# First norm's scale and bias moved from the end of the gate/up loop to units 3 to 6, on VectorE alone, and w_down's preparation two to three units later

## The chip, the cores and the metric

One core of a Trainium2 chip runs the whole program. The metric is the device time of one execution in microseconds (us). Engines are named as the profile names them: PE is TensorE's matmuls and PEld its weight loads, DVE is VectorE, ACT is ScalarE, POOL is GpSimd, SP is SyncE, which here only issues DMAs (SPq in rows).

## The reference, cut to what matters

```python
def _layernorm(x, g, b):
    mu = mean(x); var = mean((x - mu) ** 2)
    return (x - mu) * rsqrt(var + LN_EPS) * g + b
...
x = _layernorm(DN_ALPHA * x + gate_m * mix, ln1_g, ln1_b)
h = x * (1.0 + scale_f) + shift_f
ff = (silu(h @ w_gate) * (h @ w_up)) @ w_down
x = _layernorm(DN_ALPHA * x + gate_f * ff, ln2_g, ln2_b)
```

There are 2048 tokens of width 1024 in float32; the inner width of the last product pair is 2816 (22 times 128). What the change moves is two pieces of this: `* ln1_g + ln1_b` on the residual (the `x` of the last line; the `h` that feeds the products gets its scale elsewhere), and the preparation of `w_down`.

## The kernel before, in words

**Products.** Every float32 matrix is split in two float16 halves (`split`, or a copy on ACT and a subtraction on DVE), and a product is three matmuls (`mm3`, L135 to L137). The large products go by a seven-product scheme (Strassen-Winograd), so weights and activations are also added and subtracted block by block before the split, mostly on POOL.

**The gate/up loop** (`for q in range(2, NFF)`, units 0 to 21, 128 of the 2816 columns each). Unit q calls `gu` twice: `gu(q, 1)` for the second half of the tokens, then `gu(q, 0)` for the first. I call these the unit's first and second half. Each is seven products of 12 matmuls; PE runs them as A11, S2, S1, A12 and A22 (in either order), S3, S4. First halves use the PSUM tiles `mm`, second halves `ax`, four banks each. DVE's L1459 has to be done before product S3, which adds into the same bank; L1469 reads that bank after S3, L1471, L1472, L1474 and L1476 finish the half, and L1480 stores it to DRAM (`uscr`) on SP's queue. Beside the products, unit q loads the weights of unit q+3 (`gu_load`, L1384), takes the maxima of those of unit q+2 (`gu_max`, L87 into `m`), scales them (`gu_scale`) and splits those of unit q+1 (L1406, L1407, L1420, L1421). The halves' weights are held twice, so a split has a whole unit before it is needed.

**w_down** passes twice through one page of SBUF (`wd_stage["pg"]`). First `wd_load` and `wd_max` for each of 11 pieces of 1 MB (L1494, and L87 into `wdm`): three pieces per unit in units 4 to 7. After the last of them `wd_scale` reduces the 11 maxima and those of `gfrow` (L1504), and needs a maximum over the partitions for it: `all_max` lays the column out by a matmul with the identity (L99) and reduces that on DVE (L104). Then `wd_split` runs once per unit, in units 8 to 18: a multiply (L1516), four POOL additions (L1517 to L1520), two copies on ACT (L1523), two subtractions on DVE (L1524), and seven stores to `wscr` (L1526). A piece is loaded again for this.

**The first norm's scale and bias.** The normalized rows lie in DRAM as eight pieces of 1 MB (`yscr[j]`), without `ln1_g` and `ln1_b`. `y_gain(j)` loads a piece, multiplies on DVE (L1611), adds on POOL (L1612) and stores it back. Two of the eight are called in unit 19, six in unit 20. The last stage reads them as the residual.

**What sets the order.** Instructions of one engine and issues of one DMA queue run in the order in which they stand there. That order is made when the program is built, by a scheduler with its own idea of times; it moves an instruction ahead of others whose inputs come later. `with tc.high_priority()` (in `scale_of`) puts a chain first. `tc.issue_after(ins)` keeps what is issued in its block behind `ins` on `ins`'s engine: with the store of a half, a load may not pass this store on SP's queue. Otherwise the scheduler hoists: w_down's first pass of before runs in units 1 to 3, as its loads wait for nothing.

**The last stage** (after the loop) multiplies by w_down, adds into the residual and does the second norm.

Of the kernel before, what the change touches and what calls it, by code (L numbers as in the profile page):

```python
# [18 lines left out]
P = 128  # L19
T = 2048  # L20
D = 1024
# [5 lines left out]
NFF = 22  # L27
NCH = 11
# [12 lines left out]
def kernel(ctx: ExitStack, tc: tile.TileContext, xT, x, c, adaN, adaT, ada_b, w_ret, w_conv,  # L41
                             conv_w, w_out, ln1, ln1c, w_gu, w_dn, ln2, rope, consts, out):
    nc = tc.nc
# [13 lines left out]
    def page(dt=F32, at=0):  # L57


        t = unused.pop(max(-len(unused), min(at, len(unused) - 1)))  # L60
        v = t if dt == F32 else t.bitcast(dt)
        owner[id(v)] = (v, t)
        return v

    def free(*views):
        for v in views:
            unused.append(owner.pop(id(v))[1])

    def t2k(dt=F32):
        count[0] += 1  # L70
        return tmp.tile([P, 516 if dt == F32 else 1032], dt, tag="t2k", name=f"t2k{count[0]}")
# [14 lines left out]
    def absmax(dst, src):  # L86
        return nc.vector.tensor_reduce(dst, src, axis=AX.X, op=OP.max, apply_absolute_value=True).ins  # L87
# [45 lines left out]
    def mm3(ps, l_hi, l_lo, r_hi, r_lo, start, stop, again=False):  # L133

        nc.tensor.matmul(ps, l_hi, r_hi, start=start, stop=False, skip_group_check=again)  # L135
        nc.tensor.matmul(ps, l_hi, r_lo, start=False, stop=False, skip_group_check=again)  # L136
        return nc.tensor.matmul(ps, l_lo, r_hi, start=False, stop=stop, skip_group_check=again).ins  # L137
# [938 lines left out]
    for t in range(4, NT):  # L1076
        p = t // 2 + 1
# [91 lines left out]
    for b in range(2):  # L1169
        for u in range(6):  # L1170
            n = 6 * b + u
# [79 lines left out]
    def ln_rows(src):  # L1251
        pg = page()
        nc.sync.dma_start(pg.rearrange("p (a n) -> p a n", a=2),
                          bass.AP(tensor=src.tensor, offset=src.offset, ap=[[0, P], [D, 2], [1, D]]))
        return pg
# [61 lines left out]
    def plane_view(b, pl):  # L1317
        return planes[b][pl].rearrange("p (j a k n) -> p j a k n", j=4, a=2, k=4)
# [60 lines left out]
    gu_pages = ([], [], [])  # L1379
    s32 = []  # L1380
# [46 lines left out]
    def gu_done(q):  # L1427
        wa, ws = gu_w.pop(q)["pages"]
        gu_pages[0].append(wa)
        gu_pages[1].append(ws)  # L1430

    u32, ucount = [], [0]
    uscr = [[dram.tile([2, P, NCH, 512], F32, name=f"uscr{b}{r}") for r in range(2)] for b in range(2)]
    um = const.tile([P, 2, NFF], F32, name="um")

    def gu(q, bl, between=None):

        w = gu_w[q]
        iv_g, iv_u = gu_iv[q][:, 0:1], gu_iv[q][:, 1:2]
        if not u32:  # L1440
            u32.append(page())
        u = u32[0].rearrange("p (f h n) -> p f h n", f=2, h=2)[:, ucount[0] % 2]
        new = (bank, aux)[ucount[0] % 2]
        ucount[0] += 1

        def prod(ps, a, pl, start, stop):
            b = plane_view(bl, pl)
            o = ps.rearrange("p (j n) -> p j n", n=P)
            for k in range(4):
                mm3(o, w[a][:, 0, k], w[a][:, 1, k], b[:, :, 0, k], b[:, :, 1, k],  # L1450
                    start and k == 0, stop and k == 3, not start)

        pa, pb, pc = new(), new(), new()
        p1, u2 = t2k()[:, :512], t2k()[:, :512]
        e5 = w["tmp"]
        prod(pa, "A11", B11, True, True)
        nc.scalar.activation(p1, pa, AF.Copy)
        prod(pb, "S2", T2, True, True)
        nc.vector.tensor_add(u2, pb, p1)  # L1459
        prod(pc, "S1", T1_, True, True)  # L1460
        nc.scalar.activation(e5, pc, AF.Copy)
        if between:
            between()
        prod(pa, "A12", B21, False, True)
        nc.scalar.activation(u[:, 0], pa, AF.Silu, scale=iv_g)
        pd = new()
        prod(pd, "A22", T4, True, True)
        prod(pb, "S3", T3, False, True)
        nc.vector.tensor_add(p1, pb, p1)  # L1469
        nc.gpsimd.tensor_add(e5, e5, p1)  # L1470
        nc.vector.tensor_add(p1, pd, p1)  # L1471
        nc.vector.scalar_tensor_tensor(u[:, 0], p1, iv_u, u[:, 0], op0=OP.mult, op1=OP.mult)  # L1472
        prod(pc, "S4", B22, False, True)
        nc.vector.tensor_add(u2, pc, u2)  # L1474
        nc.scalar.activation(u[:, 1], u2, AF.Silu, scale=iv_g)  # L1475
        nc.vector.scalar_tensor_tensor(u[:, 1], e5, iv_u, u[:, 1], op0=OP.mult, op1=OP.mult)  # L1476

        absmax(um[:, bl, q:q + 1], u.rearrange("p h n -> p (h n)"))
        r, k = divmod(q, NCH)
        nc.sync.dma_start(uscr[bl][r][:, :, k].rearrange("h p n -> p h n"), u)  # L1480

# [5 lines left out]
    wd_stage = {}  # L1489

    def wd_load(k):
        if "pg" not in wd_stage:
            wd_stage["pg"] = page()
        nc.sync.dma_start(wd_stage["pg"], w_dn[k])  # L1494
# [14 lines left out]
    def wd_split(k):  # L1509
        if "out" not in wd_stage:  # L1510
            wd_stage["out"] = page(F16)
        f = wd_stage["pg"].rearrange("p (s n) -> p s n", s=4)
        sv = s32[0].rearrange("p (s n) -> p s n", s=4)
        o = wd_stage["out"].rearrange("p (s a n) -> p s a n", s=4, a=2)
        v = wd_stage["pg"].rearrange("p (r n) -> p r n", r=2)
        nc.vector.tensor_mul(v, v, gfrow[:, None, :].to_broadcast([P, 2, D]))  # L1516
        nc.gpsimd.tensor_sub(sv[:, 0], f[:, 1], f[:, 0])  # L1517
        nc.gpsimd.tensor_sub(f[:, 1], f[:, 3], f[:, 1])
        nc.gpsimd.tensor_sub(sv[:, 1], f[:, 3], sv[:, 0])
        nc.gpsimd.tensor_sub(sv[:, 2], f[:, 2], sv[:, 1])  # L1520
        for src, ms in ((f, (0, 6, 1, 2)), (sv[:, :3], (4, 5, 3))):
            n = len(ms)
            nc.scalar.activation(o[:, :n, 0], src, AF.Copy)  # L1523
            nc.vector.tensor_sub(o[:, :n, 1], src, o[:, :n, 0])  # L1524
            for i, m in enumerate(ms):
                nc.sync.dma_start(wscr[m][k // 4, :, k % 4], o[:, i])  # L1526
# [19 lines left out]
    def p2_xload(b, quad, c):  # L1546
        h, r = HALVES[quad]
        X[b, quad, c] = page()
        nc.sync.dma_start(X[b, quad, c].rearrange("p (k n) -> p k n", k=4)[:, :width(c)],
                          uscr[b][r][h, :, 4 * c:4 * c + width(c)])  # L1550
# [54 lines left out]


    def y_gain(j):
        pg = gu_pages[2].pop(0)
        v = pg.rearrange("p (a n) -> p a n", a=2)
        nc.sync.dma_start(v, yscr[j].rearrange("a p n -> p a n"))  # L1610
        nc.vector.tensor_mul(v, v, lnp1[0][:, None, :D].to_broadcast([P, 2, D]))  # L1611
        nc.gpsimd.tensor_add(v, v, lnp1[0][:, None, D:].to_broadcast([P, 2, D]))  # L1612
        nc.sync.dma_start(yscr[j].rearrange("a p n -> p a n"), v)
        gu_pages[2].append(pg)

    def p2_add(ps, b, m, p):
        for h, n in INTO[m]:
# [30 lines left out]
    lnp1, lnp2 = [], []  # L1648
# [77 lines left out]
    def p2_ahead(i, n, f):  # L1726
        while ns[i] < min(n, len(steps)):
            f(*steps[ns[i]])
            ns[i] += 1

    for q in range(2, NFF):
        end = q == NFF - 1
        if end:
            free(*gu_pages[0], *gu_pages[1], *gu_pages[2], *s32, *lnp1)
            for c in range(3):
                p2_xload(1, 11, c)
            p2_ahead(1, 3, p2_wload)
        gu(q, 1)
        if end:
            free(*planes[1].values())  # L1740
            for quad in (22, 21):
                for c in range(3):
                    p2_xload(1, quad, c)
        else:
            gu_split1(q + 1)
            gu_split2(q + 1, nc.gpsimd)
            if q + 3 < NFF:
                gu_load(q + 3)
            if q + 2 < NFF:
                gu_max(q + 2)  # L1750
                gu_scale(q + 2)
        if q == 3:
            wd_load(0)
        for k in range(3 * (q - 4), min(3 * (q - 4) + 3, NCH)) if q >= 4 else ():
            wd_max(k)
            wd_load((k + 1) % NCH)
            if k == NCH - 1:
                wd_scale()
        if 8 <= q < 8 + NCH:
            wd_split(q - 8)  # L1760
            if q < 7 + NCH:
                wd_load(q - 7)
        if q == NFF - 3:
            free(wd_stage["pg"], wd_stage["out"])
            gu_pages[2].append(page())
            lnp1.append(ln_rows(ln1))
        if q == NFF - 3:
            for j in (4, 5):
                y_gain(j)
        if q == NFF - 2:  # L1770
            for j in (6, 7, 0, 1, 2, 3):
                y_gain(j)
        gu(q, 0, (lambda: (p2_scale(1), p2_ahead(0, 2, p2_split))) if end else None)
        gu_done(q)
    free(*planes[0].values(), *gu_pages[0][-1:], *gu_pages[1][-1:], *u32)
    for h in range(2):
        for i in range(2):
# [116 lines left out]
```

## Time and profile before

| | us |
|---|---|
| median of 3 runs | 2124.27 (2122.6 to 2130.06) |
| the profiled execution | 2129.92 |
| its span, first to last instruction | 2128.1 |
| PE busy in it | 2026.9 (95%) |
| DVE / POOL / ACT busy | 1461.7 / 953.9 / 666.7 |

The rows of the trace come from this one execution; 1.8 us of its time lie outside its span. A row of the timeline has the start, the duration, the engine and line, what is written and read, and in brackets how long the engine idled before it and what ended this. The page's list by fortieths of the span shows where PE has gaps: near the start, around 900 us, and from 1600 to 1700 us.

### The profile page before, as it was taken

To read this page: it belongs to the slowest core of one execution; us is meant where nothing else is said; L and a number is where in the kernel's file an instruction comes from. 1 tells how busy PE (TensorE), PEld (TensorE's weight loads), DVE (VectorE), ACT (ScalarE), POOL (GpSimd) and SP (SyncE) were. 2 spreads that over 40 slices of the span, in tenths; PEclk is the share of its full clock that TensorE was granted. 3 is DMA by queue.
4 is the path that set the end of the run, shared out by engine and by line. 5 is a ranking of instruction groups with operands and counts; after the bars stand their busy time and mean duration, and the time that the engine had idled before them with its cause. 6 is when DMAs were issued, how large, how long until landed. Compare 5 with 4: busy or idle time off the path is not lost.

```text
span 2128.1 us, 24625 instructions
## 1 busy us (share of the span) xinstructions
PE 2026.9 (95%) x9631; PEld 949.7 (45%) x9631; DVE 1461.7 (69%) x1769; ACT 666.7 (31%) x728; POOL 953.9 (45%) x759
## 2 busy tenths in 40 slices
PE   8899898989899999799999999999999899999998
PEld 4355444444444544344444444444444344444443
DVE  7899556667677577768745677777767454378564
ACT  5522443424322222323323233333432122122210
POOL 3554655555742277733312344444447333134232
PEclk9999999999999999999999999999999999999999
DMA  9047454586684288765411234343345874475311
GB/s 375 25 136 237 129 159 109 150 263 190 219 315 168 82 236 200 176 180 205 149 50 60 98 131 144 126 141 134 135 167 203 298 309 175 157 271 189 149 71 78
DMA packets 189492, 361.06 MB, mean 170 GB/s; under 512 B 118080, under 2 KB 118080, under 8 KB 166592
## 3 DMA queue, kind: packets, MB, share of 16 engines
q1 hardware_dynamic: 181168, 344.55, 48.3%
q10 hardware_dynamic: 8208, 14.95, 2.0%
q8 instruction: 75, 1.23, 0.2%
q14 instruction: 41, 0.34, 0.0%
HBM read 231.26 MB, written 100.93 MB: 156 GB/s over the span
## 4 chain that ended last, share of the span: by engine, by line
PE 47%; DVE 5%; POOL 4%; DMA 4%; issue 2%; ACT 1%; SPq 0%; POOLq 0%; DVEq 0%; ACTq 0%
PE ax L135 8%; PE ax L136 8%; PE ax L137 8%; PE mm L135 8%; PE mm L136 8%; PE mm L137 8%; DMA pg<-in_w_dn_dram 1%; POOL pg L1612 1%; DMA pg<-yscr 1%; DMA yscr<-pg 1%; DVE wdm L87 1%; ACT pg L1272 1%; DVE pg L1611 1%; DVE pg L1335 1%; POOL pg L1336 1%
## 5 line engine op out<-in xcount | busy, mean ns | idle before, releaser
L135 PE MATMUL mm<-pg,pg 128*128 128x512 f16 x1604 | 608.6, 381 | 23.2 <-ACT pg L1420 8.2
L136 PE MATMUL mm<-pg,pg 128*128 128x512 f16 x1604 | 611.1, 381 | 0.0
L137 PE MATMUL mm<-pg,pg 128*128 128x512 f16 x1604 | 610.2, 381 | 0.5 <-DVE pg L889 0.5
L135 PE MATMUL ax<-pg,pg 128*128 128x512 f16 x1220 | 463.1, 380 | 12.4 <-DVE pg L1301 2.9
L136 PE MATMUL ax<-pg,pg 128*128 128x512 f16 x1220 | 463.2, 380 | 0.0
L137 PE MATMUL ax<-pg,pg 128*128 128x512 f16 x1220 | 461.6, 380 | 0.6 <-DVE pg L889 0.6
L135 PEld LDWEIGHTS <-pg 128*128 128x128 f16 x2888 | 284.1, 98 | 362.9 <-DMA pg<-pg 16.0
L136 PEld LDWEIGHTS <-pg 128*128 128x128 f16 x2888 | 284.1, 98 | 356.1 <-issue 30.4
L137 PEld LDWEIGHTS <-pg 128*128 128x128 f16 x2888 | 283.9, 98 | 350.3 <-issue 18.8
L1470 POOL TENSOR_TENSOR pg<-pg,t2k 128x512 f32<-128x512 f32 x44 | 57.9, 1317 | 328.6 <-DVE x L114 194.0
L131 DVE SCALAR_TENSOR_TENSOR pg<-pg,p2s,pg 128x2048 f16<-128x2048 f32 (+1 forms) x42 | 92.7, 2216 | 138.1 <-ACT pg L130 138.0
L130 ACT ACTIVATE pg<-pg,p2s 128x2048 f16<-128x2048 f32 (+1 forms) x42 | 77.5, 1858 | 262.3 <-PE mm L136 114.1
L1407 DVE TENSOR_TENSOR pg<-pg,pg 128x2048 f16<-128x2048 f32 x22 | 50.3, 2286 | 69.8 <-ACT pg L1406 69.8
L87 DVE TENSOR_REDUCE m<-pg 128x2 bf16<-128x2048 f32 (+1 forms) x38 | 86.3, 2276 | 16.2 <-DMA pg<-in_w_gu_dram 10.0
L525 PE MATMUL mm<-pg,pg 128*128 128x512 f16 x384 | 91.1, 393 | 5.6 <-DVE pg L533 2.5
L1475 ACT ACTIVATE pg<-t2k,ivg 128x512 f32<-128x512 f32 x44 | 31.5, 716 | 174.3 <-DVE t2k L1474 174.3
L1523 ACT ACTIVATE pg<-pg 128x2048 f16<-128x2048 f32 (+1 forms) x22 | 37.3, 1697 | 107.8 <-DMA wscr<-pg 69.6
L1524 DVE TENSOR_TENSOR pg<-pg,pg 128x2048 f16<-128x2048 f32 (+1 forms) x22 | 44.4, 2016 | 38.8 <-ACT pg L1523 38.8
L131 DVE SCALAR_TENSOR_TENSOR pg<-pg,hs,pg 128x1024 f16<-128x1024 f32 x32 | 48.5, 1535 | 29.2 <-ACT pg L130 29.0
L1264 POOL TENSOR_SCALAR rs<-mv 128x1 f32<-128x1 f32 x32 | 30.5, 957 | 82.2 <-DVE mv L1262 79.6
L1577 POOL TENSOR_TENSOR pg<-pg,pg 128x2048 f32<-128x2048 f32 (+1 forms) x6 | 26.9, 4490 | 82.0 <-DVE pg L131 38.6
L525 PEld LDWEIGHTS <-pg 128*128 128x128 f16 x384 | 38.0, 101 | 53.8 <-issue 10.0
(278 smaller groups left out, 2834.6 us busy)
## 6 DMA issues: line engine op xcount, KB each, us to landing
pg<-wscr SPq DMA_DIRECT2D x28, 1024.0 KB, 5.0
pg<-in_w_gu_dram SPq DMA_DIRECT2D x22, 1024.0 KB, 4.8
uscr<-pg SPq DMA_DIRECT2D x44, 512.0 KB, 2.7
pg<-in_w_dn_dram SPq DMA_DIRECT2D x22, 1024.0 KB, 5.8
pg<-in_adaT_dram SPq DMA_DIRECT2D x21, 1024.0 KB, 7.2
wscr<-pg SPq DMA_DIRECT2D x77, 256.0 KB, 2.9
yscr<-pg SPq DMA_DIRECT2D x16, 1024.0 KB, 4.9
pg<-uscr SPq DMA_DIRECT2D x16, 1024.0 KB, 6.5
```

Of the source, the lines that this page charges most:

```text
L87: return nc.vector.tensor_reduce(dst, src, axis=AX.X, op=OP.max, apply_absolute_value=True).ins
L130: nc.scalar.activation(hi, src, AF.Copy, scale=s)
L131: nc.vector.scalar_tensor_tensor(lo, src, s, hi, op0=OP.mult, op1=OP.subtract)
L135: nc.tensor.matmul(ps, l_hi, r_hi, start=start, stop=False, skip_group_check=again)
L136: nc.tensor.matmul(ps, l_hi, r_lo, start=False, stop=False, skip_group_check=again)
L137: return nc.tensor.matmul(ps, l_lo, r_hi, start=False, stop=stop, skip_group_check=again).ins
L525: nc.tensor.matmul(ps, hv[:, a, k, o], w[:, k], start=n == 0 and k == k0, stop=n == 2 and k == k1 - 1)
L1407: nc.vector.tensor_sub(wa[:, 2048:], pg, wa[:, :2048])
L1470: nc.gpsimd.tensor_add(e5, e5, p1)
L1475: nc.scalar.activation(u[:, 1], u2, AF.Silu, scale=iv_g)
L1523: nc.scalar.activation(o[:, :n, 0], src, AF.Copy)
L1524: nc.vector.tensor_sub(o[:, :n, 1], src, o[:, :n, 0])
```

## The change

`y_gain` now works in one page of its own (with a second page for `ln1`'s rows), does all four passes on DVE (a multiply and an addition for each half of the piece, 128x1024), and is called twice per unit in units 3 to 6: once behind the store of the unit's first half, once behind that of its second half (`tc.issue_after(gu_last[0])`). w_down's maxima are taken in units 7 to 9 (four, four and three), each load behind the store of the half before it; its splits run in units 10 to 20.

```diff
-    u32, ucount = [], [0]
+    u32, ucount, gu_last = [], [0], [None]
...
-        nc.sync.dma_start(uscr[bl][r][:, :, k].rearrange("h p n -> p h n"), u)
+        gu_last[0] = nc.sync.dma_start(uscr[bl][r][:, :, k].rearrange("h p n -> p h n"), u).ins
...
     def y_gain(j):
-        pg = gu_pages[2].pop(0)
-        v = pg.rearrange("p (a n) -> p a n", a=2)
+        v = lnp1[1].rearrange("p (a n) -> p a n", a=2)
         nc.sync.dma_start(v, yscr[j].rearrange("a p n -> p a n"))
-        nc.vector.tensor_mul(v, v, lnp1[0][:, None, :D].to_broadcast([P, 2, D]))
-        nc.gpsimd.tensor_add(v, v, lnp1[0][:, None, D:].to_broadcast([P, 2, D]))
+        for a in range(2):
+            nc.vector.tensor_mul(v[:, a], v[:, a], lnp1[0][:, :D])
+            nc.vector.tensor_add(v[:, a], v[:, a], lnp1[0][:, D:])
         nc.sync.dma_start(yscr[j].rearrange("a p n -> p a n"), v)
-        gu_pages[2].append(pg)
...
-            free(*gu_pages[0], *gu_pages[1], *gu_pages[2], *s32, *lnp1)
+            free(*gu_pages[0], *gu_pages[1], *gu_pages[2], *s32, wd_stage["pg"], wd_stage["out"])
...
-        if q == 3:
-            wd_load(0)
-        for k in range(3 * (q - 4), min(3 * (q - 4) + 3, NCH)) if q >= 4 else ():
+        with tc.issue_after(gu_last[0]):
+            if q == 3:
+                lnp1.extend((ln_rows(ln1), page()))
+            if 3 <= q < 7:
+                y_gain((4, 6, 0, 2)[q - 3])
+        for k in range(4 * (q - 7), min(4 * (q - 7) + 4, NCH)) if q >= 7 else ():
             wd_max(k)
-            wd_load((k + 1) % NCH)
+            with tc.issue_after(gu_last[0]):
+                wd_load((k + 1) % NCH)
             if k == NCH - 1:
                 wd_scale()
-        if 8 <= q < 8 + NCH:
-            wd_split(q - 8)
-            if q < 7 + NCH:
-                wd_load(q - 7)
-        if q == NFF - 3:
-            free(wd_stage["pg"], wd_stage["out"])
-            gu_pages[2].append(page())
-            lnp1.append(ln_rows(ln1))
-        if q == NFF - 3:
-            for j in (4, 5):
-                y_gain(j)
-        if q == NFF - 2:
-            for j in (6, 7, 0, 1, 2, 3):
-                y_gain(j)
+        if 10 <= q < 10 + NCH:
+            wd_split(q - 10)
+            if q < 9 + NCH:
+                wd_load(q - 9)
         gu(q, 0, (lambda: (p2_scale(1), p2_ahead(0, 2, p2_split))) if end else None)
         gu_done(q)
+        with tc.issue_after(gu_last[0]):
+            if 3 <= q < 7:
+                y_gain((5, 7, 1, 3)[q - 3])
+            if q == 6:
+                free(*lnp1)
+                wd_load(0)
```

Three places show how the change moves instructions.

**Place A, DVE where the first half of unit 4 runs.** Before (the rows from unit 4's weights' successor maximum to the end of the half; `t2k` are scratch tiles, `mm` the PSUM tiles of the half):

```order
L87 TENSOR_REDUCE m_8106<-pg_76 128x2
L87 TENSOR_REDUCE um<-pg_75 128x1
L1459 TENSOR_TENSOR t2k_7760<-mm_7757,t2k_7759 128x512
L1469 TENSOR_TENSOR t2k_7759<-mm_7757,t2k_7759 128x512
L1471 TENSOR_TENSOR t2k_7759<-mm_7813,t2k_7759 128x512
```

Changed:

```order
L87 TENSOR_REDUCE m_8124<-pg_76 128x2
L87 TENSOR_REDUCE um<-pg_75 128x1
L1459 TENSOR_TENSOR t2k_7772<-mm_7769,t2k_7771 128x512
L1611 TENSOR_TENSOR pg_92<-pg_92,pg_80 128x1024 x2
L1612 TENSOR_TENSOR pg_92<-pg_92,pg_80 128x1024 x2
L1469 TENSOR_TENSOR t2k_7771<-mm_7769,t2k_7771 128x512
L1471 TENSOR_TENSOR t2k_7771<-mm_7825,t2k_7771 128x512
```

The four passes on a piece (`pg_92`) stand between L1459 and L1469 in first halves; in second halves they stand between L1459 and the split's L1407.

**Place B, DVE at the end of w_down's maxima.** Before, in unit 3:

```order
L1459 TENSOR_TENSOR t2k_7526<-mm_7523,t2k_7525 128x512
L87 TENSOR_REDUCE wdm<-pg_80 128x1
L87 TENSOR_REDUCE um<-pg_75 128x1
L87 TENSOR_REDUCE x_8607<-wdm 128x1
L87 TENSOR_REDUCE x_8608<-gfrow 128x1
L1504 TENSOR_TENSOR m_8609<-x_8607,x_8608 128x1
L1469 TENSOR_TENSOR t2k_7525<-mm_7523,t2k_7525 128x512
```

Changed, in unit 9 (`mm_8987`, `mm_8988` and `mm_9043` are the first half's tiles):

```order
L87 TENSOR_REDUCE wdm<-pg_80 128x1
L1469 TENSOR_TENSOR t2k_8989<-mm_8987,t2k_8989 128x512
L1474 TENSOR_TENSOR t2k_8990<-mm_8988,t2k_8990 128x512
L1471 TENSOR_TENSOR t2k_8989<-mm_9043,t2k_8989 128x512
L1476 SCALAR_TENSOR_TENSOR pg_75<-pg_91,ivg_8629,pg_75 128x512
L1472 SCALAR_TENSOR_TENSOR pg_75<-t2k_8989,ivg_8629,pg_75 128x512
L87 TENSOR_REDUCE um<-pg_75 128x1
L87 TENSOR_REDUCE wdm<-pg_80 128x1 x2
L87 TENSOR_REDUCE x_9122<-wdm 128x1
L87 TENSOR_REDUCE x_9123<-gfrow 128x1
L1504 TENSOR_TENSOR m_9124<-x_9122,x_9123 128x1
```

The last two maxima stand behind the end of unit 9's first half; on SP's queue their two loads stand right behind the store of that half.

**Place C, PE where the maximum's column (`m`) is laid out by L99.** Before, in unit 8's first half, five units after L1504:

```order
L135 LDWEIGHTS pg_91
L135 MATMUL mm_8474<-pg_78,pg_91 128x512
L99 LDWEIGHTS m_8609
L99 MATMUL ax_8615<-ident_105,m_8609 128x128
L136 LDWEIGHTS pg_91
L136 MATMUL mm_8474<-pg_78,pg_91 128x512
```

Changed:

```order
L137 LDWEIGHTS pg_94
L137 MATMUL mm_9244<-pg_93,pg_94 128x512
L99 LDWEIGHTS m_9124
L99 MATMUL ax_9130<-ident_105,m_9124 128x128
L135 LDWEIGHTS pg_84
L135 MATMUL ax_9139<-pg_82,pg_84 128x512
```

`mm_9244` belongs to unit 10's first half: five of its seven products (A11, S2, S1, A22, S4) now stand between unit 9's first half and L99, and all seven products of unit 9's second half (`ax_9139` and on) stand behind L99.

## Rows read from the trace of the kernel before

**Rows 1.** Windows: stretch, its length, busy PE PEld DVE ACT POOL, PEclk, DMA share, GB/s.

```profile
1000.00:1050.00 50.00, 47.89 (x224) 21.59 (x222) 34.45 (x35) 13.76 (x17) 10.00 (x9) 1.00 0.45 158
1150.00:1200.00 50.00, 50.00 (x237) 22.85 (x236) 27.16 (x33) 13.69 (x16) 9.35 (x9) 1.00 0.12 44
1600.00:1650.00 50.00, 46.11 (x207) 20.37 (x205) 37.61 (x27) 11.93 (x13) 37.48 (x14) 0.97 0.60 222
1650.00:1700.00 50.00, 44.14 (x204) 19.88 (x204) 24.45 (x23) 7.47 (x12) 16.90 (x6) 1.00 0.80 291
...
900.00:903.00 3.00, 3.00 (x9) 0.85 (x8) 3.00 (x5) 2.10 (x2) 0.00 (x0) 0.56 1.13 213
```

**Rows 2.** Waits of PE, 940 to 1760 us: total, times, longest.

```profile
PE mm L135 <- DVE t2k L1459: 6.3, 3, 2.9
PE mm L135 <- ACT t2k L1457: 3.6, 3, 2.2
PE mm L135 <- issue: 2.3, 1, 2.3
PE ax L135 <- DVE t2k L1459: 2.0, 1, 2.0
```

**Rows 3.** Timeline of PE: matmuls behind an idle stretch.

```profile
899.05 0.61 PE L135 MATMUL mm<-pg,pg 128*128 128x512 f16 x1 [8.22 <-ACT pg L1420]
...
1616.74 0.59 PE L135 MATMUL mm<-pg,pg 128*128 128x512 f16 x1 [2.91 <-DVE t2k L1459]
1617.12 0.63 PE L136 MATMUL mm<-pg,pg 128*128 128x512 f16 x1
```

**Rows 4.** Timeline of DVE and POOL in units 19 and 20.

```profile
1616.61 6.08 DVE L1611 TENSOR_TENSOR pg<-pg,pg 128x2048 f32<-128x2048 f32 x1
1651.59 5.45 DVE L1421 TENSOR_TENSOR pg<-pg,pg 128x1536 f16<-128x1536 f32 x1
...
1650.91 4.51 POOL L1612 TENSOR_TENSOR pg<-pg,pg 128x2048 f32<-128x2048 f32 x1
```

**Rows 5.** Timeline of DVE in units 5 and 6, with neither piece of work.

```profile
1123.87 2.29 DVE L1407 TENSOR_TENSOR pg<-pg,pg 128x2048 f16<-128x2048 f32 x1 [8.79 <-ACT pg L1406]
...
1137.50 0.67 DVE L1459 TENSOR_TENSOR t2k<-mm,t2k 128x512 f32<-128x512 f32 x1
1142.91 0.69 DVE L1469 TENSOR_TENSOR t2k<-mm,t2k 128x512 f32<-128x512 f32 x1 [4.74 <-PE mm L137]
...
1147.91 1.22 DVE L87 TENSOR_REDUCE um<-pg 128x1 f32<-128x1024 f32 x1
1150.75 0.69 DVE L1459 TENSOR_TENSOR t2k<-ax,t2k 128x512 f32<-128x512 f32 x1 [1.62 <-PE ax L137]
```

**Rows 6.** Timeline: w_down's maxima and one of their loads, and `gfrow`'s maximum.

```profile
1008.21 2.29 DVE L87 TENSOR_REDUCE wdm<-pg 128x1 f32<-128x2048 f32 x1 [0.83 <-DMA pg<-in_w_dn_dram]
1015.67 2.29 DVE L87 TENSOR_REDUCE wdm<-pg 128x1 f32<-128x2048 f32 x1 [5.18 <-DMA pg<-in_w_dn_dram]
...
1034.92 1.20 DVE L87 TENSOR_REDUCE x<-gfrow 128x1 f32<-128x1024 f32 x1
```

**Rows 7.** Timeline of SP's issues in units 4 to 6.

```profile
1010.52 0.33 SPq L1494 DMA_DIRECT2D pg<-in_w_dn_dram  x1
...
1089.85 0.35 SPq L1384 DMA_DIRECT2D pg<-in_w_gu_dram  x1
1097.91 13.98 SPq L1480 DMA_DIRECT2D uscr<-pg  x2
1126.23 0.34 SPq L1384 DMA_DIRECT2D pg<-in_w_gu_dram  x1
1134.28 13.98 SPq L1480 DMA_DIRECT2D uscr<-pg  x2
```

**Rows 8.** DMA issues over the whole span: KB each, median us to landing.

```profile
pg<-in_w_dn_dram SPq DMA_DIRECT2D x22, 1024.0 KB, 5.8
...
yscr<-pg SPq DMA_DIRECT2D x16, 1024.0 KB, 4.9
...
pg<-yscr SPq DMA_DIRECT2D x8, 1024.0 KB, 5.6
```

**Rows 9.** Chain of work that ended last: start, us, what.

```profile
1604.60 7.35 DMA pg<-yscr
```

**Rows 10.** Groups by line: busy us, mean ns of one, idle before.

```profile
L1611 DVE TENSOR_TENSOR pg<-pg,pg 128x2048 f32<-128x2048 f32 x8 | 23.1, 2884 | 17.3 <-DMA pg<-yscr 12.8 <-DMA pg<-in_ln_dram 4.5
L1612 POOL TENSOR_TENSOR pg<-pg,pg 128x2048 f32<-128x2048 f32 x8 | 40.1, 5011 | 35.5 <-DVE pg L1611 35.5
```

## The prediction

> **What bounds the kernel now.** PE. I read first the share of each engine (PE 95%), then the windows of 50 us from the start of the gate/up loop on, then PE's waits, then the timeline behind each wait. From 1050 to 1600 us every window shows PE busy for 50.00 of 50 us; [rows 1] shows one of them, and the three that are not so: 2.1 us are missing in 1000 to 1050, 3.9 in 1600 to 1650 and 5.9 in 1650 to 1700. The waits [rows 2] name the causes: DVE's L1459 and ACT's L1457 come late; only the 2.3 us "issue" lie earlier, in unit 1, and are not touched. So what this change can give back is these 11.9 us, and what follows a wait: behind the 2.91 us at 1616.74 matmuls start 0.43 apart instead of the usual 0.215 [rows 3], for some 6.6 of them, 1.4 us (the window's PEclk is 0.97). Sum 13.3 us, 0.6% of the time. About 0.5% is what a measurement of this kernel can tell from no change.
>
> **Why PE waits in 1600 to 1700.** POOL's addition takes 5.0 us a piece [rows 10], and DVE's passes run into it: L1611 took 6.08 at 1616.61, L1421 took 5.45 beside POOL's 4.51 [rows 4]. Between them DVE waits for pieces to land, and L1459 stands behind. In 1000 to 1050 w_down's maxima do the same: DVE waits 5.18 us for one load [rows 6] with the half's work behind it.
>
> **The change, part by part.** I count from t = 0, the start of unit 7's first half. A unit lasts 36.37 us (weight loads at 1089.85 and 1126.23 [rows 7]), a half 18.18, a product 2.59. The half whose second product ends L1459's wait at 1150.75 [rows 5] began 2 x 2.59 before 1150.7, at 1145.5, so first halves begin at 1127.3 and every 36.37 from there; t = 0 is 1163.7 of before. PE needs L1459 before S3, five products in, 12.95 after a half's start.
>
> *Removed at the end:* all 9.8 us of waits and the 1.4 of slow clock. What is late there next? Splits of w_down, which in units 8 to 18 run beside the products at no cost in PE (windows at 50.00). I take the whole. If the last two splits should hold the last stage's first weights, half of it is left.
>
> *Removed in units 1 to 3:* the maxima, hence 2.1 us. DVE then has the load of 1150 to 1200, 27.2 of 50 us [rows 1].
>
> *Added in units 3 to 6, eight times:* a load of 5.6 and a store of 4.9 us [rows 8], four DVE passes. One of 128x2048 took 2.3 with POOL idle, so these are 1.15 each, 4.6 a piece (place A of the order). In a first half the load is issued behind the store at 1134.28 [rows 7] and lands at 1140.2; DVE idles there until 1142.91 [rows 5]; the passes end at 1144.8 and L1469 is 1.9 late. Nobody on PE waits: the four `mm` banks are next written a unit later, and `um` ends before L1459 of the next half is due. In a second half the load waits for the earlier store to land and for the half's store, lands some 28 us after the first half's start, and its passes end at 32.7; L1407 would begin at 33.0 (1123.87 + 36.37 - 1127.3) [rows 5], and DVE idles 8.79 before it. L1459 of the next first half ends 10.9 after that half's start, 2.0 before it is due. Price 0; above, at 7.35 a load [rows 9], 1 to 2 us a unit; a gain has no ground, since nothing there waits now.
>
> *Moved to units 7 to 9: eleven maxima.* From a load's issue at 1010.52 to the maximum at 1015.67 are 5.15 us, the maximum is 2.3, a cycle 7.46 [rows 6, 7]. With one page the loads form a chain, and DVE stands still in it, since maxima are in its order ahead of the halves' work. Followed row by row through the order: passes of the eighth piece end at 17.5; load 0 lands at 23.1, max 0 ends 25.7, max 1 33.1, max 2 40.6; then L1474, L1471, L1421, the weights' maximum, L1472, L1476, and L1459 of unit 8's first half ends at 47.7, due at 49.3: 1.6 to spare. Max 3 ends at 50.0, max 4 at 57.4, the half's store is issued at 61.7 and load 5 behind it; max 6 ends at 76.9, L1459 of unit 9's first half at 84.2, due 85.7: 1.5 to spare. Max 8 ends at 93.9, and behind it stand L1469 and the rest of that half, so its store is issued at 98.1. Loads 9 and 10 stand behind this store (place B): max 9 ends at 105.9, max 10 at 113.3. The reductions of `wdm` and `gfrow` (1.20 [rows 6]) and L1504 make it 115.0.
>
> *The new wait.* PE ends unit 9's first half at 90.9 (5 x 18.18). Of unit 10's products ahead of L99 (place C) S2 needs the bank that L1469 reads until 94.5, at 93.4: 1.1 us. Five products later, at 105.0, PE stands at L99, whose column is ready at 115.0: **10.0 us**, with unit 9's second half behind it. In before L1504 was done at 1036 and L99 stood five units later; this slack is what the move spends. Bounds: if the half's store came as early as in before (2.5 us behind PE, 93.4), 5 to 6.5 us; with loads at 5.8 [rows 8], some 13. I take 10.0, from the row of this very load in a calm stretch. After such an idle (8.22 us at 899.05 [rows 3]) the granted clock was 0.56 in the next 3 us [rows 1], the lower level of 1.2 GHz: eight matmuls at 0.43, 1.7 us. Behind it DVE has L1516 and its backlog, but L1459 of the next two halves is by the same count 6 us ahead of its due time. Then the splits run as in before.
>
> *A price from a page.* The Trainium skill's page "DMA: Bandwidth & Descriptors", section "Bandwidth", lists 6.15 us for 1 MB from HBM (issued from GpSimd, which is not so here). By that the three waits would be some 5 us longer and the time 2129; the rows of this load show 5.15, and these count.
>
> *Sum.* Gone 2.1 + 9.8 + 1.4 = 13.3. New 1.1 + 10.0 + 1.7 = 12.8. Net -0.5 on the profiled 2129.9, so 2129.4; this execution was 5.65 above the median, hence 2124.27 - 0.5, about **2124**.
>
> **The rivals.**
>
> *PE does not wait at L99.* Then 13.3 less 1.1 at most are gained: 2124.3 - 12.5 = 2112. This happens if the maxima are done some 8 us sooner than I count, or if PE lets the ready products of unit 9's second half (18 us of work, operands there since unit 8) pass the waiting row. Against the second: at 1616.74 PE stood idle for 2.91 us for one product [rows 3]. The Trainium skill's "TensorE: Matmul & The Clock Gate", section "Architectural detail: the array is 16× 32×32, not 1× 128×128", calls PE's queue a partial reorder window that pulls weight loads ahead of matmuls; by that alone L99's weight load could be passed, and the time would be this rival's. The trace agrees only with the matmuls' staying in order. Chance 0.09.
>
> *Slower: DVE held by loads in every half.* The spare times of 1.6 and 1.5 us cover three loads each, so from 0.5 us more per load on (5.65) S3 waits. At 7.35, as with the y load at 1604.60 [rows 9], three loads are 6.6 late: waits of 5.0, 5.1 and 6.6 more at L99, three slow clocks instead of one (3.4): 2124 + 20 = 2144. For it: load, weights and stores share one queue. Against: DMA share is 0.12 in 1150 to 1200 and 0.45 where 5.15 was measured [rows 1]. Chance 0.09.
>
> *The end does not clear.* The splits of units 19 and 20 or their stores hold the last stage's first weights, and half of the 11.2 stays: 2130, still within 0.5%. Chance 0.08.
>
> **How the numbers follow.** My forecast, that the waits at the end are traded for one at L99, has 0.74; its own bounds are 2118 (L99 at 5.5) to 2130 (13, and some S3 wait). The range reaches from 2115 to 2133: it leaves out the first two rivals. Faster by over 0.5% (below 2113.7) takes the first rival and little else, 0.09; slower (above 2134.9) the second and the tail of the third, 0.12; the rest, 0.79, is within.
>
> **What would show it.** In the changed profile PE's windows from 1600 to 1700 show 50.00; L1611 and L1612 stand on DVE between about 1060 and 1190, four per piece, with waits on `yscr` but none of PE behind them; DVE shows 4 to 5 us of idle on in_w_dn before some of the eleven maxima between 1185 and 1280; and PE shows one idle of about 10 us near 1265 to 1277, released by DVE's L1504, with PEclk below 1 behind it, and about 1 us some 12 us ahead of it. Wrong if that idle is below 5 or above 14, if S3 waits in units 4 to 9 sum to over 3 us, or if anything is left at the end.

## The result, and the profile after

| | before | after |
|---|---|---|
| median, runs | 2124.51 (2122.6 to 2130.06), 4 | 2138.95 (2138.19 to 2141.97), 4 |
| ratio, 95% interval | | 1.0063 (1.0047 to 1.0078) |
| profiled execution's span | 2128.1 | 2136.4 |

The change costs 0.63%, 14.4 us between the medians; 2124 was forecast, with a range to 2133. The two spans differ by 8.3 only. The rest lies ahead of the change: the weights of the second unit of the gate/up loop were loaded at 942.93 in the profiled execution of before and at 937.76 in that of after. From there to the span's end are 1185.2 and 1198.6 us, so the loop and what follows it are 13.4 us longer, which fits the medians. In what follows times are counted within the loop.

Windows of after (length, busy PE, PEld, DVE, ACT, POOL, PEclk, DMA share, GB/s):

```profile
1000.00:1050.00 50.00, 50.00 (x237) 22.77 (x235) 28.43 (x31) 15.54 (x17) 10.08 (x9) 1.00 0.29 110
1050.00:1100.00 50.00, 47.83 (x222) 21.49 (x221) 38.53 (x38) 14.71 (x18) 17.74 (x15) 1.00 0.48 175
...
1150.00:1200.00 50.00, 49.59 (x234) 22.51 (x233) 36.26 (x34) 15.13 (x16) 10.57 (x9) 1.00 0.51 185
1200.00:1250.00 50.00, 48.13 (x225) 21.73 (x224) 38.12 (x37) 14.53 (x17) 11.28 (x13) 1.00 0.45 168
1250.00:1300.00 50.00, 37.35 (x164) 16.36 (x163) 23.71 (x28) 6.84 (x8) 5.71 (x6) 0.90 0.32 110
1300.00:1350.00 50.00, 47.62 (x222) 21.44 (x220) 39.78 (x35) 20.18 (x21) 27.02 (x21) 1.00 0.50 169
1350.00:1400.00 50.00, 47.78 (x218) 21.34 (x216) 38.51 (x33) 17.92 (x19) 22.63 (x15) 0.97 0.37 127
...
1600.00:1650.00 50.00, 50.00 (x235) 22.69 (x234) 36.25 (x32) 17.60 (x19) 23.90 (x16) 1.00 0.42 141
1650.00:1700.00 50.00, 50.00 (x234) 22.63 (x232) 25.33 (x26) 12.98 (x14) 9.62 (x7) 1.00 0.58 191
```

Beside [rows 1]: 1000 to 1050 and 1600 to 1700 are full now. What was to be given back, was. In its place PE loses 2.2 us in 1050 to 1100 (units 4 and 5), 2.3 in 1150 to 1250, 12.7 in 1250 to 1300, and 4.6 in 1300 to 1400. PE starts unit 7 at 1158.50 and unit 9 at 1233.17.

PE's waits of after, 940 to 1780 us (total, times, longest), against [rows 2]:

```profile
PE ax L99 <- DVE m L1504: 10.3, 1, 10.3
PE mm L135 <- DVE t2k L1459: 4.8, 5, 1.5
PE ax L135 <- ACT t2k L1457: 2.9, 2, 2.2
PE mm L135 <- DVE t2k L1469: 2.3, 1, 2.3
PE mm L135 <- ACT t2k L1457: 1.1, 1, 1.1
```

The forecast wait stands first, with 10.3 us where 10.0 were predicted. On the timeline (PE, DVE, then SyncE's issues):

```profile
1257.20 0.38 PE L135 MATMUL mm<-pg,pg 128*128 128x512 f16 x1 [2.31 <-DVE t2k L1469]
...
1278.07 0.29 PE L99 MATMUL ax<-ident,m 128*128 128x128 f16 x1 [10.34 <-DVE m L1504]
```

```profile
1267.10 2.29 DVE L87 TENSOR_REDUCE wdm<-pg 128x1 f32<-128x2048 f32 x1 [5.29 <-DMA pg<-in_w_dn_dram]
1274.20 2.29 DVE L87 TENSOR_REDUCE wdm<-pg 128x1 f32<-128x2048 f32 x1 [4.82 <-DMA pg<-in_w_dn_dram]
...
1277.85 0.16 DVE L1504 TENSOR_TENSOR m<-x,x 128x1 bf16<-128x1 f32 x1
```

```profile
1250.79 10.16 SPq L1480 DMA_DIRECT2D uscr<-pg  x2
1261.05 15.80 SPq L1494 DMA_DIRECT2D pg<-in_w_dn_dram  x3
```

The last two maxima wait 5.29 and 4.82 us for loads that SyncE issues only behind the store of unit 9's first half (the second store of the merged row; of the three loads behind it the third is the first split's), and PE stands until L1504. Behind the idle the granted clock was 0.50, the lower level of 1.2 GHz (0.56 in [rows 1]), and came back:

```profile
1279.00:1282.00 3.00, 3.00 (x9) 1.07 (x8) 1.60 (x4) 0.00 (x0) 0.22 (x1) 0.50 0.54 227
1282.00:1285.00 3.00, 3.00 (x13) 1.33 (x12) 1.66 (x1) 1.08 (x2) 0.00 (x0) 0.84 0.00 0
```

A group of three matmuls takes 1.28 us there instead of 0.65; four groups, from 1278.15 to 1283.12, take 4.97 instead of 2.59: 2.4 us.

What was not forecast stands in units 10 and 11 (PE, ACT, POOL):

```profile
1331.60 0.38 PE L135 MATMUL mm<-pg,pg 128*128 128x512 f16 x1 [1.12 <-ACT t2k L1457]
1338.01 0.38 PE L135 MATMUL mm<-pg,pg 128*128 128x512 f16 x1 [1.06 <-DVE t2k L1459]
1353.34 0.38 PE L135 MATMUL ax<-pg,pg 128*128 128x512 f16 x1 [2.22 <-ACT t2k L1457]
```

```profile
1317.79 1.48 ACT L1523 ACTIVATE pg<-pg 128x1536 f16<-128x1536 f32 x1 [6.66 <-DMA wscr<-pg]
...
1328.97 1.48 ACT L1420 ACTIVATE pg<-pg 128x1536 f16<-128x1536 f32 x1 [6.84 <-POOL pg L1417]
...
1330.97 0.58 ACT L1457 ACTIVATE t2k<-mm 128x512 f32<-128x512 f32 x1
...
1347.57 1.48 ACT L1523 ACTIVATE pg<-pg 128x1536 f16<-128x1536 f32 x1 [8.26 <-DMA wscr<-pg]
1352.08 0.72 ACT L1475 ACTIVATE pg<-t2k,ivg 128x512 f32<-128x512 f32 x1 [3.02 <-DVE t2k L1474]
1352.71 0.58 ACT L1457 ACTIVATE t2k<-ax 128x512 f32<-128x512 f32 x1
```

```profile
1321.15 3.29 POOL L1415 TENSOR_TENSOR pg<-pg 128x512 f32<-128x512 f32 x1 [6.03 <-DVE pg L1524]
1324.51 3.20 POOL L1416 TENSOR_TENSOR pg<-pg,pg 128x512 f32<-128x512 f32 x1
```

For the wait at 1331.60, L1457 stands on ACT behind L1420 of the next weights' split. This waits for POOL's L1415 to L1417, and L1415 for L1524 of w_down's split, whose second copy (L1523) had to wait for the first three stores to leave the page (the third landed at 1317.69). For the longest wait, at 1353.34, the chain is another: L1457 stands on ACT behind L1475. This waits for DVE's L1474, and L1474 stands on DVE behind the second L1524 of the next split, which waits 6.38 us for its copy (L1523), and the copy waits 8.26 us for the stores again. In before ACT has the two the other way round, and the wait of L1475 holds nobody up:

```profile
1220.89 0.60 ACT L1457 ACTIVATE t2k<-ax 128x512 f32<-128x512 f32 x1 [1.01 <-PE ax L137]
1225.80 0.72 ACT L1475 ACTIVATE pg<-t2k,ivg 128x512 f32<-128x512 f32 x1 [4.31 <-DVE t2k L1474]
```

The three waits and a fourth of 0.2 are 4.6 us, and a second stretch of slow clock behind 1353.34 (granted 0.61 in 1354 to 1357; three groups of matmuls in 3.63 us instead of 1.94) makes 1.7.

### The profile page after: what moved, and what is told of

Its sections match the earlier page's. It is cut to its first block, busy times and chain, and to the rows that moved or that the text cites. A ratio compares the mean times of both kernels' runs of the same rounds, so it can differ in the third digit from the quotient of the medians.

```text
span 2136.4 us, 24635 instructions
## 1 busy us (share of the span) xinstructions
PE 2029.5 (95%) x9631; PEld 950.0 (44%) x9631; DVE 1472.9 (69%) x1793; ACT 666.8 (31%) x728; POOL 910.4 (43%) x751
## 4 chain that ended last, share of the span: by engine, by line
PE 42%; DVE 9%; DMA 5%; POOL 4%; issue 2%; ACT 1%; SPq 0%; POOLq 0%; DVEq 0%; ACTq 0%
PE ax L135 7%; PE ax L136 7%; PE ax L137 7%; PE mm L135 7%; PE mm L136 7%; PE mm L137 7%; DMA pg<-yscr 2%; DMA pg<-in_w_dn_dram 2%; DVE pg L1611 1%; DVE wdm L87 1%; DVE pg L1476 1%; DVE pg L1612 1%; ACT pg L1272 1%; DVE pg L1335 1%; DVE pg L1472 1%
## 5 line engine op out<-in xcount | busy, mean ns | idle before, releaser
L135 PE MATMUL ax<-pg,pg 128*128 128x512 f16 x1220 | 465.8, 382 | 12.3 <-ACT t2k L1457 5.1
L135 PEld LDWEIGHTS <-pg 128*128 128x128 f16 x2888 | 284.5, 99 | 362.0 <-DMA pg<-pg 13.4
L1475 ACT ACTIVATE pg<-t2k,ivg 128x512 f32<-128x512 f32 x44 | 31.5, 717 | 173.2 <-DVE t2k L1474 173.2
L1407 DVE TENSOR_TENSOR pg<-pg,pg 128x2048 f16<-128x2048 f32 x22 | 52.2, 2374 | 43.3 <-ACT pg L1406 43.3
L1524 DVE TENSOR_TENSOR pg<-pg,pg 128x2048 f16<-128x2048 f32 (+1 forms) x22 | 46.2, 2099 | 44.5 <-ACT pg L1523 44.5
L1523 ACT ACTIVATE pg<-pg 128x2048 f16<-128x2048 f32 (+1 forms) x22 | 37.3, 1696 | 104.5 <-DMA wscr<-pg 71.0
```

The source lines that it names most:

```text
L1407: nc.vector.tensor_sub(wa[:, 2048:], pg, wa[:, :2048])
```

## The experiments

All ratios are against the kernel before, timed beside the run; its medians lay between 2125.4 and 2126.0 there.

**e0, the kernel before once more.**

> The kernel before, profiled once more, because its first profile was of an execution of 2129.9 us while the median is 2124.5. If the traced execution was an ordinary one, this one shows the same waits in 1600 to 1700 us (9.8 us) and in 1025 to 1031 (2.1 us) and reaches unit 6 at about 1127 us. If part of the 5.4 us above the median lay ahead of the gate/up loop, unit 6 starts some 3 to 5 us sooner here and the waits at the end are the same. If it lay at the end, the waits in 1600 to 1700 are only 4 to 7 us, and this change had less to give back than 11.2 us.

2127.28 us (one run). From the same load of weights to the end it took 1184.8 us, 1185.2 in the first profile; the waits between 940 and 1780 sum to 11.3 us beside "issue", 11.9 in [rows 2]. So the account of the loop in before holds in a second execution, and most of the 2.7 us between the two spans lies ahead of the loop.

**e1, w_down's scale later.**

```diff
-            if k == NCH - 1:
-                wd_scale()
...
         gu_done(q)
+        if q == 9:
+            wd_scale()
```

> The changed kernel with w_down's scale written behind unit 9's second half instead of ahead of it, so that the matmul that lays out its column (L99) stands behind twelve products of unit 9's second and unit 10's first half, not behind five of unit 10's first half. Theory A: the place of L99 costs its own wait (10.3 us), the wait of product S2 of unit 10 for L1469 (2.3) and the slow clock behind it (2.1); without them 2139 - 14.7 = 2124 us. If the waits in units 10 and 11 (4.5 us and 1.8 of slow clock) hang on the disturbed order of the products as well, 2118. Theory B: L99 only shows that DVE is late by the loads of w_down; the lateness appears at the next products S3 or at the first split instead, and the time stays at 2135 or above.

2124.65 us, ratio 0.9996 (0.9987 to 1.0005): 14.3 us less than the changed kernel, 14.7 expected by A. No wait stands at L99, and none for L1469. That settles the largest part: the place of the scale's chain, and in it of one 128x128 matmul in PE's order (the edit moves the chain's instructions on DVE as well). In units 10 and 11 the first split still comes late here (L1516 at 1291.17), and PE waits 4.3 us for one L1457, so the further gain that A allowed for, down to 2118, did not come:

```profile
PE mm L135 <- ACT t2k L1457: 4.7, 2, 4.3
PE mm L135 <- DVE t2k L1459: 4.3, 6, 1.6
```

**e2, without w_down's first pass**.

```diff
-        for k in range(4 * (q - 7), min(4 * (q - 7) + 4, NCH)) if q >= 7 else ():
...
+        if q == 9:
+            nc.vector.memset(wd_m[:, :NCH], 0.125)
+            wd_scale()
```

> The changed kernel without w_down's first pass: the eleven loads and maxima are left out and a constant stands for them, the rest is as in the changed kernel, with y's scale and bias in units 3 to 6 on DVE. Theory A (all of the loss is the first pass, as placed, and its column): the waits at the end stay away and nothing is new, 2139 less 14.7, 6.2 and the 1.9 us of waits for L1459 in units 8 and 9, so 2114 to 2117 us. Theory C (the passes on y are not free in units 3 to 6, they cost 1 us or more in each unit): 2120 us or more, with waits of PE for L1457 or L1459 between 1040 and 1190 us.

2114.25 us, 0.9944 (0.9930 to 0.9957). One row is left of PE's waits between 1040 and 1780 us:

```profile
PE mm L135 <- DVE t2k L1459: 1.2, 2, 0.6
```

So y's passes in units 3 to 6 are nearly free (1.2 us of waits in units 5 and 7), the splits in units 10 to 20 are free where nothing ahead of them is late, and 24.7 us of the changed kernel's time come with the first pass in units 7 to 9.

**e3, the addition at the end on DVE.**

```diff
-        nc.gpsimd.tensor_add(v, v, lnp1[0][:, None, D:].to_broadcast([P, 2, D]))
+            nc.vector.tensor_add(v[:, a], v[:, a], lnp1[0][:, D:])
```

> The kernel before with one edit: at the end of the gate/up loop the addition of the bias is done on DVE instead of POOL, in the four passes of the changed kernel; where and when the pieces are loaded stays. If POOL's additions (5.0 us a piece, with DVE's passes drawn out beside them) make the 9.8 us of waits in 1600 to 1700, the most of them go: 2113 to 2117 us. If the loads of y make them (DVE standing behind a piece that has not landed), nothing much changes: 2122 to 2126 us.

2123.22 us, 0.9989 (0.9980 to 0.9997). In 1600 to 1700 PE still loses 6.3 of the 9.8 us, in two waits. Ahead of one (3.1 us) DVE idles 3.52 us for a piece to land. Ahead of the other (3.2 us) it runs without a gap, with y's multiplies in its row. So about a third goes with POOL's additions, although DVE has their work now; how the rest divides between the loads and the passes themselves is not settled. Nothing in the forecast hung on that, as all of it goes.

**e4, a second page for the first pass.**

```diff
-                wd_load((k + 1) % NCH)
+                if k + 2 < NCH:
+                    wd_first(k + 2)
...
```

(`wd_first` loads into one of two pages in turn; the second is given back before the first split.)

> The changed kernel with a second page for w_down's first pass (the page that the splits take later), so that the load of piece k+2 waits for the maximum of piece k and not for that of k+1; L99 keeps its place on PE and the loads stay behind the halves' stores, of which only the load of the last piece now stands behind that of unit 9's first half. Theory A (the chain of one load, one maximum through one page makes both the lateness of L1459 and the wait at L99): one cycle of 7.1 us and the 2 us of waits for L1459 are gained, 2139 - 9 = 2130 us, with 1 to 4 us left at L99. Theory D (the loads' own time is the limit, two in flight take twice as long): 2137 us or more and still 9 us or more at L99.

2133.36 us, 1.0031 (1.0020 to 1.0042): 5.6 of the 9 us. The wait at L99 fell as A expects, to

```profile
1273.73 0.29 PE L99 MATMUL ax<-ident,m 128*128 128x128 f16 x1 [3.16 <-DVE m L1510]
```

but four maxima now stand in one half ahead of L1459 (in unit 7 from 1198.87 to 1213.5), and PE waits 5.8 us for L1459 in place of 4.8.

**e5, the edits of e1 and e4 together.**

```diff
+                if k + 2 < NCH:
+                    wd_first(k + 2)
...
+        if q == 9:
+            wd_scale()
...
```

> Both edits at once: a second page for w_down's first pass, and its scale behind unit 9's second half. In the run with the scale late alone some 9 us of new waits were left, 5 of them in units 10 and 11, where ACT's copies and L1457 stood behind a first split that came late. Theory E (the first split is late because the last maxima are late, and that alone makes the waits of unit 10): with the maxima done some 7 us sooner they go, 2114 to 2118 us. Theory F (they come from the split's own order on ACT, copy behind store, whatever the maxima do): 2121 us or more, with 4 us or more of waits for L1457 between 1300 and 1350 us.

2123.14 us, 0.9984 (0.9975 to 0.9994), the time that F gave, and yet not F: in 1300 to 1350 PE waits only 0.5 us, and not for L1457. E is right on units 10 and 11 and missed the time, but the waits for L1459 and L1457 in units 4 to 9 sum to 8.3 us here (up to 2.7 at once), which I had not counted in either.

**e6, the first pass stays early, y's passes in units 4 to 7.**

```diff
+            if q == 4:
+                free(wd_stage.pop("pg"))
+                lnp1.extend((ln_rows(ln1), page()))
+            if 4 <= q < 8:
+                y_gain((4, 6, 0, 2)[q - 4])
+        if q == 3:
+            wd_load(0)
+            for k in range(NCH):
...
+        if 9 <= q < 9 + NCH:
+            wd_split(q - 9)
...
```

> The other way to share the pages: w_down's first pass stays in units 1 to 3 as in the kernel before, the passes on y take its page and the splits' page in units 4 to 7, on DVE as in the changed kernel, and the splits run in units 9 to 19. Theory A: the 2.1 us of waits in units 1 to 3 stay, the 11.2 us at the end go, the passes on y cost 1 us as in the run without maxima: 2125 - 11 + 1 = 2115 us. Rival: the splits, which end a unit later than before, or the passes on y in unit 7 beside the first split, hold units 7 to 9 as in the changed kernel: 2120 us or more.

2112.77 us, 0.9938 (0.9924 to 0.9953), faster than both kernels: the 11.2 us at the end are gone, the waits of units 1 to 3 are there (2.2), and every window of 50 us from 1050 to 1700 that was read is full, as these two:

```profile
1000.00:1050.00 50.00, 47.84 (x225) 21.68 (x224) 34.89 (x43) 14.50 (x16) 9.90 (x10) 1.00 0.37 132
1050.00:1100.00 50.00, 50.00 (x235) 22.74 (x234) 35.41 (x36) 15.65 (x19) 17.14 (x15) 1.00 0.42 155
```

**e7, the loads of units 7 to 9 not held.**

```diff
-            with tc.issue_after(gu_last[0]):
-                wd_load((k + 1) % NCH)
+            wd_load((k + 1) % NCH)
```

> The changed kernel with w_down's loads of units 7 to 9 no longer held behind the halves' stores; the page, the scale and L99's place stay. On SyncE's queue one of the last two loads now stands ahead of the store of unit 9's first half. Theory A (the last two loads wait for that store, and L99 for them): the wait at L99 becomes 4 to 7 us shorter, the slow clock behind it stays: 2132 to 2135 us. If the hold made nothing late (the page's chain alone sets the last maximum): 2138 to 2140 us.

2129.65 us, 1.0017 (1.0008 to 1.0025): 9.3 us gained, more than the 4 to 7 of A. L99 runs at its place in the order without any wait:

```profile
1259.42 0.58 PE L135 MATMUL mm<-pg,pg 128*128 128x512 f16 x1 [2.26 <-DVE t2k L1469]
1271.37 0.22 PE L99 MATMUL ax<-ident,m 128*128 128x128 f16 x1
```

```profile
1267.63 0.16 DVE L1504 TENSOR_TENSOR m<-x,x 128x1 bf16<-128x1 f32 x1
```

L1504 runs at 1267.63 instead of 1277.85, in two profiles that issue a load of weights in unit 7 at 1160.04 (after) and 1160.24. In after PE stood at L99 from 1267.73 on, so without the hold nearly the whole wait goes; e4 shows that a second page takes 7.2 us of it as well, so hold and single page make it together. A counted the hold of the last two loads alone, but it acts in unit 8 too: there after issues a load at 1224.01, behind the store at 1223.54, though the page was free at 1219.5, and its maximum comes at 1229.59 where e7 has it at 1224.85. The 4.6 us of waits in units 10 and 11 (2.1, 1.2, 1.1 and 0.2) have stayed.

**e8, e6 with a second page** (the edit against e6).

```diff
-                if k + 1 < NCH:
-                    wd_load(k + 1)
+                if k + 2 < NCH:
+                    wd_first(k + 2)
```

> The kernel with the first pass left in units 1 to 3 and the passes on y in units 4 to 7 (2112.8 us), with the second page for w_down's first pass. If DVE standing behind one page makes the 2.1 us of waits in units 1 to 3, they go: 2110 to 2112 us. Rival, from the two runs with a second page in units 7 to 9: the maxima then stand in pairs and in fours ahead of L1459 and PE waits for it by 2 us in a half, so nothing is gained or 2 to 4 us are lost: 2113 to 2117 us.

2112.77 us, 0.9939 (0.9925 to 0.9953). The 2.1 us in units 1 to 3 went, as expected, but 2.1 us came up in another place, a y piece of unit 7 with DVE idle 6.41 us before it. What the second page is worth by itself this one profile does not settle; in time it is nothing.

**e9, e1 and e7 together.**

```diff
-            with tc.issue_after(gu_last[0]):
-                wd_load((k + 1) % NCH)
+            wd_load((k + 1) % NCH)
...
+        if q == 9:
+            wd_scale()
```

> The changed kernel with the scale behind unit 9's second half and the loads of units 7 to 9 not held. Theory G (the 4.6 us of waits in units 10 and 11, the same in the changed kernel, with two pages and without the hold, whether L99 waits 10, 3 or 0 us, come from the order of the products that L99's place makes, unit 10's first half ahead of unit 9's second): with the usual order and an earlier first split they go, and S2's 2.3 us too; 2129.7 - 4.6 - 1.8 - 2.3 = 2121 us or less. Theory F (they come with any first split in unit 10): 2125 us or more, with 4 us of waits between 1300 and 1350 us.

2121.49 us, 0.9984 (0.9975 to 0.9993), G's 2121 or less. 1300 to 1350 is full:

```profile
1300.00:1350.00 50.00, 50.00 (x236) 22.74 (x235) 38.83 (x32) 19.35 (x20) 22.67 (x15) 1.00 0.40 140
```

With e4, e5 and e7 this shows what the waits in units 10 and 11 hang on. Where L99 stands behind five products of unit 10 (after, e4, e7), 4.6 us of waits follow, whether L99 itself waited 10.3, 3.2 or 0 us; where it stands later and the first split is early enough (e5, e9), 0.5 or none do. The first split itself is not late in e7: L1516 starts 113.1 us behind that load of weights in unit 7, in e9 118.1. A late first split under the usual order (e1) brings waits back in another form. Of the way in which that order makes them, the rows show one link of the longest: in unit 11 of after, e4 and e7 L1457 stands behind L1475 on ACT (in e1 too, with a wait of 0.5), in e9 ahead of it, as in before. The rest is argued, not shown: five products of unit 10's first half are done early, so unit 11's come closer behind the split that L1457 stands behind on ACT.

## Why the prediction was wrong, step by step

| step | predicted | measured in the loop |
|---|---|---|
| gone at the end | 11.2 | 11.9 (units 19 and 20 last 84.39 before, 72.52 after) |
| gone in units 1 to 3 | 2.1 | 2.1 |
| y's passes, units 3 to 6 | 0 | 2.2 (0.7 and 1.5) |
| L1459 in units 7 to 9 | 0 | 2.3 (0.4, 1.2, 0.7) |
| S2 of unit 10 | 1.1 | 2.3 |
| L99 | 10.0 | 10.3 |
| slow clock behind it | 1.7 | 2.4 |
| units 10 and 11, with their slow clock | 0 | 6.3 |

New are 25.8 us and gone 14.0, net 11.8; the 13.4 between the two loops leave 1.6 unassigned.

**Right.** What bounds the kernel, what the end and units 1 to 3 gave back, and the wait at L99 with its cause, its place and its size. e1 and e7 each take it away by another handle. The size held although PE reached L99 4 us later than counted, and the column came 4.6 us later: both follow from L1469 of unit 9's first half, which ended at 1257.2 (98.7 from unit 7's start, 94.5 counted). PE stood at L99 10.5 us behind it and the column was there 20.9 us behind it, 10.5 and 20.5 in the prediction. In before L99 ran at 1166.78, in unit 7, which is four units behind L1504 and not five; nothing in the sum changes by that.

**The step that failed most: "Then the splits run as in before."** The order that I printed to place L99 (place C) also showed five products of unit 10 ahead of unit 9's second half, and I followed it only as far as the wait. Behind L99 I counted DVE's lateness alone and priced units 10 and 11 at nothing, because the splits were free in units 8 to 18 of before. That cover was the usual order of the products. In before L1417 was done at 1227.97 and L1420 came at 1236.38, 8.4 us to spare:

```profile
1226.26 1.71 POOL L1417 TENSOR_TENSOR pg<-pg,pg 128x512 f32<-128x512 f32 x1
1236.38 1.48 ACT L1420 ACTIVATE pg<-pg 128x1536 f16<-128x1536 f32 x1 [3.44 <-PE ax L136]
```

In after L1420 waits 6.84 us for L1417, and ahead of the longest wait L1457 has changed places with L1475. The term put at nothing measured 6.3 us (4.6 of waits and 1.7 of slow clock), half of the 12.3 by which the steps together were off; without it the time would be about 2133 by this count, an estimate.

**Half-steps that were followed singly.** In units 3 to 6 I put each of a unit's two passes on y against the store times of before. But each load stands behind a store that the other piece's passes have pushed back. In unit 6 of after, which starts at 1122.13:

```profile
1131.14 0.36 SPq L1480 DMA_DIRECT2D uscr<-pg  x1
...
1146.67 0.36 SPq L1480 DMA_DIRECT2D uscr<-pg  x1
...
1168.08 0.36 SPq L1480 DMA_DIRECT2D uscr<-pg  x1
```

The first store comes 9.0 behind the start (7.1 in [rows 7]), the second 24.5 (about 21), the third 9.6 behind the start of unit 7 at 1158.50. The passes of the eighth piece therefore end 20.2 us behind the start of unit 7 (the last L1612 starts at 1177.53), where I had 17.5. These 2.7 us exceed both the 1.6 and the 1.5 us of spare that I had found for units 8 and 9, by 1.1 and 1.2; the waits were 1.2 and 0.7. With 1.5 in unit 5 and 0.4 in unit 7, PE waited 3.8 us before S3 in units 4 to 9, more than the 3 that the prediction had named as a sign of being wrong. The S3 rival had the right mechanism, a spare that one late step uses up, but it looked for it in the loads alone. These were nearly as I took them: the last two maxima follow each other by 7.10 us, 7.46 taken.

**The slow clock** was taken as eight matmuls; it was twelve, and it came a second time.

**The other rivals.** PE did not pass the waiting row: 10.34 us with unit 9's second half ready behind it. The Trainium skill's "TensorE: Matmul & The Clock Gate", section "Architectural detail: the array is 16× 32×32, not 1× 128×128", speaks of weight loads that are pulled ahead. The trace shows none of that at L99: PEld idles 10.83 us before L99's weight load at 1278.06, so no weight load and no matmul behind it ran ahead. (That rival's 2112 takes off 12.5 where 13.3 less 1.1 is 12.2.) The end cleared wholly. The outcome above 2133 came from none of the rivals as priced but from three terms that I had set at zero (2.2, 2.3 and 6.3) and two that I had too small (S2 and the slow clock, 1.9 together), all on one side: those set at zero were argued from a cover in before, and the range had no room for the covers failing together.

## What to carry to other kernels

When an order is printed to find one wait, read on behind it: products that change places take the slack from everything that was placed around them, whether or not the wait itself is cured. Work that comes twice per period is to be followed as a loop, with each step's start taken from the step before it in the new kernel, until the times repeat; spares of 1 to 2 us are no spares until then. A matmul that needs a scalar's column belongs far behind the last input of the scalar, or the inputs early, as in e6; holding a chain of loads behind stores costs time at each hold when the chain's end is awaited, 9.3 us in all here (e7).

## What the runs showed of the hardware

POOL's and DVE's passes took longer where they ran side by side: in after L1415 took 3.29 us at 1321.15, beside DVE's L1516 and an L1407 of 3.35, against 1.27 in each later unit, and L1407 2.29. That one slows the other is read from the overlap; no run here parts them. The 3.20 us of L1416 behind it are nothing new: it took 3.20 in the units with a split in before too, and 1.3 to 1.6 in units without. The part ahead of the loop varied by 5 us between executions of kernels that are the same there, as much as most terms of this account, so spans of single profiles are compared only behind a common event.
